# Five small reorderings in a fused neighbourhood-attention layer: square root's table, squares, held outputs, double loads, roots

## The chip, the cores and the metric

The kernel runs on one core of a Trainium2 chip. The metric is the device time of one execution in microseconds, the median over several runs. Engines are named as the profile names them: PE is TensorE (PEld its weight loads), DVE is VectorE, ACT is ScalarE, POOL is GpSimd, SP is the engine that issues most of the DMAs.

## The reference, cut to what matters

The reference has two kinds of layers, but with `DEPTH = 1` only the first one runs. All data is float32: `x` is 2048 tokens by 1024 features, there are 16 heads of 64, and the tokens form a grid of 32 rows by 64 columns.

```python
h = rmsnorm(x, norm_0)
q, k, v, gate = split(h @ w_in_0, 4)          # 1024 x 4096 weights
# each token attends to 8 rows x 16 columns around it, with a bias per head
s = q . k / sqrt(64) + rpb_0[head, row offset, column offset]
o = softmax(s) @ v
x = x + (o * silu(gate)) @ w_out_0            # 1024 x 1024 weights
out = rmsnorm(x, norm_f)
```

`rmsnorm(x, g)` is `x * rsqrt(mean(x*x) + 1e-6) * g`, so every token needs one inverse root at the beginning and one at the end.

## The kernel before, in words

Every float32 product is made of three products of a narrower float32 form: each operand is split into a high part (a copy on ACT) and a residual (a subtraction on DVE), and PE multiplies high by high, high by low and low by high. The large projections also use a scheme with seven instead of eight half-size products, so operands are first added and subtracted (`S1` to `S4` for weights, `T1` to `T4` for `x`) and results are combined again.

The instructions are issued in an order written out by hand; each engine works through its own list in that order, and an instruction waits until its operands and its buffer are ready. Buffers come from pools of fixed size: `ev` has 8, `mp` 10, `raw` 6. A buffer is handed out again when all that reads the old tile is done.

`stage_one` projects the tokens of column chunks 0 and 1 (512 tokens each). Its list is `seq`: product `i` is a pair (unit `n`, `P`), where a unit is 128 columns of keys, queries or gates, twice. `step(i)` issues the twelve matmuls of product `i` (L447), then `after` (L494), which reads the bank, and then what `on(i, ...)` has put down for this place. Products 0 to 11 are the `P` = 1 and 2 of six units. From product 12 on the other five products of each unit follow, with units taken in pairs:

- `add` (L457, its operation at L460) reads a bank to which a later product of the same unit adds: `P` = 7 adds to the bank of `P` = 6, and so has to wait until `add` has read it.
- `out_` (L462) makes a finished output `tmp` at L465 and multiplies it by `rb[c]` at L468, the inverse root of each token of chunk `c`, spread over the partitions. On DVE for units below 6, on POOL above. As long as `rb[1]` isn't there, outputs of chunk 1 are put on the list `held`; `scale_held` scales and stores them all. `give` (L363) stores an output through SP at L380 some matmuls later.
- `first_out(n)` (L743) makes the output of `P` = 2 of unit `n`, with an operation at L360.
- `forms(i)` makes the split of the weights for the products up to `i` (L429 on ACT, L430 on DVE); `seven.sum` makes `S1` to `S4` (L436). `sums4` (L741) and `split` (L543 and L544) make `T4`.

The inverse roots of a chunk come about like this. `load_rows` (L641) loads eight half rows of tokens on SP, `square_rows` squares them on ACT with a sum (L207), `stats` (L209) adds the sums on DVE (L212, L213), takes the square root on ACT (L149) and finishes it on DVE (L150 to L153). `diagonal` puts the four results of a partition on diagonals and splits them (with `late` on ACT at L225 and L229, the residual on DVE at L232), and `spread_rstd` multiplies a matrix of ones, `onesr`, with both parts on PE (L241, L242), which spreads them over all partitions, and copies the result to `rb[c]`.

ACT evaluates functions from a table that it has to load (ACT_TABLE_LOAD in the profile). Copies and squares run without a load of their own once a table is there.

Attention runs in 32 cycles, each with the transposes of one pair of heads and 512 tokens (`ph`, L1342), their copies `pta` (L1331 on DVE, L1333 on ACT), the scores of the next (`s`, L1287), and the products with the values (`o`, L1361). Between them `feed` issues matmuls of projections or, later, of the output projection (`po`, L1565 to L1569), so that PE has work. Within a cycle, once its attention weights are normalised (`normalise`, L1312 on DVE), some of these may be issued:

- `split_rows`, which splits one tile of 128 rows of attention outputs for the output projection (L1407 on ACT, L1408 on DVE, two each),
- `run_scales`, which multiplies finished rows with their inverse root (two operations at L1479 on DVE) and sends them to the output,
- `run_roots`, which makes the final inverse root of a finished tile by eight operations on one column (L1464 to L1471 on DVE). It isn't run where scaling was due in the same cycle (`behind`).

`add_rows` adds the residual to a finished output product (L1437 on DVE), with a square on ACT a few matmuls later (L1440). The last ten tiles of rows follow after attention in `rows_by_seven` (`py`, L1657).

Of the kernel before, what the change touches and what calls it, by code (L numbers as in the profile page):

```python
# [11 lines left out]
F32 = mybir.dt.float32  # L12
# [65 lines left out]
def build(ctx, tc, x, xr, xt, wg, bias, w_out, n0, nf, out):  # L78
# [59 lines left out]
    ones = one.tile([128, 128], F32, name="ones")  # L138
    nc.vector.memset(ones, 1.0)
    onesr = one.tile([128, 128], F32R, name="onesr")  # L140
    rt = one.tile([128, 16], F32, name="rt")
    rth = one.tile([128, 8], F32, name="rth")
    g0 = one.tile([128, NK], F32, name="g0")
# [270 lines left out]
    def seven_products(us, c0, X1, also):  # L414
        seq = [(n, P) for n in range(len(us)) for P in order7]
        last = len(us) - 1
        A, F, B, U = {}, {}, {}, {}
        made, held = [0], []

        def load_w(n, f, home=raw):  # L420
            A[n, f] = home([128, 512], F32, "raw")
            k, j = us[n]
            b = 512 * quarter[f]
            nc.sync.dma_start(A[n, f], wg[KINDS[k] + j, :, b:b + 512])

        def form(n, P):
            src = A[n, uses[P][0]]
            F[n, P] = t = wp([128, 2, 512], F32R, "f")
            nc.scalar.activation(t[:, 0], src, AF.Copy)  # L429
            nc.vector.tensor_tensor(t[:, 1], src, t[:, 0].bitcast(F32), OP.subtract)  # L430

        def sum_(n, f):
            a, b, o = {"S1": ("A21", "A22", OP.add), "S2": ("S1", "A11", OP.subtract),
                       "S3": ("A11", "A21", OP.subtract), "S4": ("A12", "S2", OP.subtract)}[f]
            A[n, f] = xp([128, 512], F32, "s") if f in ("S1", "S2") else A[n, {"S3": "A21", "S4": "A12"}[f]]
            nc.vector.tensor_tensor(A[n, f], A[n, a], A[n, b], o)  # L436

        def product(n, P):
            if P in (1, 6, 5):
                B[n, P] = bank(512, "pp")  # L440
                for Q in {1: (2,), 6: (7, 4), 5: (3,)}[P]:
                    B[n, Q] = B[n, P]
            x, t = X1[uses[P][1]], F.pop((n, P))
            for k in range(4):
                c = slice(k * 128, k * 128 + 128)
                for m in range(3):
                    nc.tensor.matmul(B[n, P], t[:, int(m == 2), c], x[k][int(m == 1)],  # L447
                                     start=P in (1, 6, 5) and k == 0 and m == 0, stop=k == 3 and m == 2,
                                     skip_group_check=True)
                    due(1)  # L450

        def keep(n, home=None):
            kind = us[n][0]
            U[n, 1] = home or ep([128, 512], F32, "p1")
            nc.scalar.activation(lay(kind, U[n, 1]), of(kind, B[n, 1]), AF.Copy)

        def add(n, i, P):  # L457
            kind = us[n][0]
            U[n, i] = xp([128, 512], F32, "u")
            nc.vector.tensor_tensor(lay(kind, U[n, i]), of(kind, B[n, P]), lay(kind, U[n, 1]), OP.add)  # L460

        def out_(n, a, c, P, u, then):  # L462
            kind, j = us[n]
            tmp = ev([128, 512], F32, "tmp")
            nc.vector.tensor_tensor(lay(kind, tmp), of(kind, B[n, P]), lay(kind, u), OP.add)  # L465
            def scale():
                if c0 == 0:
                    (nc.vector if n < 6 else nc.gpsimd).tensor_tensor(tmp, tmp, rb[c], OP.mult)  # L468

            if c0 == 0 and c not in rb:  # L470
                held.append(lambda: (scale(), give(kind, 2 * j + a, c, tmp)))
                return
            scale()
            then.append(lambda: give(kind, 2 * j + a, c, tmp))

        def scale_held():
            while held:
                held.pop(0)()

        def ahead(i, lead=6):  # L480
            n, j = divmod(i, 7)
            if j == 5 and n + 2 <= last:
                for f in ("A21", "A22", "A11"):
                    load_w(n + 2, f)
            if j == 0 and n + 1 <= last:
                load_w(n + 1, "A12")
            while made[0] < len(seq) and made[0] <= i + lead:
                form(*seq[made[0]])
                made[0] += 1
            f = {0: "S1", 1: "S2", 2: "S3", 4: "S4"}.get(j)  # L490
            if f and n + 1 <= last:
                sum_(n + 1, f)

        def after(n, P, then):  # L494
            kind, j = us[n]
            if P == 1:
                keep(n)
            elif P == 6:
                add(n, "2", 6)
            elif P == 2:  # L500
                if c0 == 0:
                    evac(kind, 2 * j, c0, B[n, 2], then)
                else:
                    then.append(lambda kind=kind, j=j, p=B[n, 2]: give(kind, 2 * j, c0, p, True))
            elif P == 7:
                add(n, "3", 7)
            elif P == 5:
                out_(n, 1, c0 + 1, 5, U[n, "3"], then)
            elif P == 4:
                out_(n, 1, c0, 4, U[n, 1], then)  # L510
            elif P == 3:
                out_(n, 0, c0 + 1, 3, U[n, "2"], then)

        def run():
            then = []
            for i, (n, P) in enumerate(seq):
                product(n, P)
                now, then = then, []
                after(n, P, then)
                for f in now:  # L520
                    f()
                ahead(i)
                also(n - last, i - 7 * n)
            for f in then:
                f()

        parts = SimpleNamespace(load=load_w, form=form, sum=sum_, product=product, keep=keep, after=after, scale_held=scale_held, B=B)
        return ahead, run, parts

# [86 lines left out]
    def stage_one():  # L616
# [24 lines left out]
        def load_rows(c, hs, p):  # L641
            for h in hs:
                t, j = 4 * c + h // 2, h % 2
                rows_in[t, j] = p([128, 512], F32, "row")
                nc.sync.dma_start(rows_in[t, j], xr[t * 128:t * 128 + 128, 512 * j:512 * j + 512])
# [55 lines left out]
        def on(i, f, *a):  # L701
            todo.setdefault(i, []).append((f, a))
# [44 lines left out]
        parts_ = slice(0, 256), slice(256, 512)  # L747
        load_v0(0, 0, 0, cols=parts_[0], by=nc.scalar)
        load_x(0, "x11", 0, land["x11"][0], parts_[0])
        nc.scalar.activation(onesr, ones, AF.Copy)  # L750
        load_v0(0, 1, 0, cols=parts_[0])
        load_x(0, "x11", 0, land["x11"][0], parts_[1])
        load_v0(0, 0, 0, cols=parts_[1])
# [54 lines left out]
        for n in (4, 5):  # L808
            seven.load(n, "A11")
        load_rows(1, range(4), ev)  # L810
        load_rows(1, range(4, 6), mp)
        for k in range(4, 8):
            first_values(k)
            split("B22", "x22", (k - 4,), "x22")
# [27 lines left out]
            for f in ("S1", "S2"):  # L842
                seven.sum(n, f)
        split("T2", "x11", (1, 2))
        square_rows(1, range(2))
        step(7)
        split("T2", "x11", (3,))
        square_rows(1, range(2, 4))
        load_rows(1, range(4, 8), ev)
        for n in range(2):  # L850
            seven.sum(n, "S3")
        step(8)
# [10 lines left out]
        step(11)  # L863
        sums4(0, 1)
        forms(15)
        for k in range(4):
            if k < 2:
                on(12 + k, sums4, k + 2)
            on(12 + k, split, "T4", "x21", (k,))
        on(12, square_rows, 1, range(4, 8))  # L870
        on(14, seven.sum, 0, "S4")
        on(14, first_out, 2)
        on(13, stats, 1)
        on(16, seven.sum, 1, "S4")
        on(16, first_out, 3)
        on(15, diagonal, 1, ev, True)
        on(17, spread_rstd, 1)
        on(18, seven.scale_held)

        def ask_pair(a):  # L880
            spot = mkp([128, 3, 512], F32, "raw")
# [908 lines left out]
    for m in range(cycles + 1):  # L1790
# [3 lines left out]
        if m:  # L1794
            due_here = []
            quiet[0] = True
            if a < 12 and m > 8 and m % 2:
                normalise(2 * m - 1, True, lambda: due_here.append(split_rows() or consume(1, turn=True)))
            else:
                normalise(2 * m - 1, True)  # L1800
            most, behind = 99 if a > 12 else 0 if rows_due() else 1, bool(rooted)
            run_scales()
            if not behind:
                run_roots(most)
            for k in range(3):
                if m == 1 and k == 2:
                    pass
                elif a > 12 or not any(due_here) and (k < 1 or k < 2 and m > 8 and m % 2 == 0):
                    got = split_rows()
                    due_here.append(got)  # L1810
                    if not got:
                        consume(1, turn=True)
                    elif a < 12 and m % 2 == 0 and len(items) - state["used"] == 8:
                        feed(a * 0.2)
                        consume(1, turn=True)
                feed(a * 0.2)
        else:
            feed(a * 0.6)
# [61 lines left out]
```

## Time and profile before

| | us |
|---|---|
| median of 3 runs | 1009.08 (1009.04 to 1009.55) |
| the profiled execution: time | 1008.7 |
| the profiled execution: span from the first to the last instruction | 1006.6 |
| PE busy in the span | 996.1 |
| DVE busy | 772.9 |
| ACT busy | 521.6 |
| POOL busy | 149.6 |

PE's granted clock is 0.998 of full speed. In the rows of the timeline the columns are the start in us from the beginning of the span, the length in us, the engine, the line, the operation, what it writes and reads, the shape and the count; in brackets stands how long the engine was idle before it, and what ended that. A group of rows that overlap, as they do on all engines, is shorter from start to start than its lengths add up to. In the rows of waits stand the engine that waited, its line, the engine and line that ended the wait, the total in us, how often, and the longest. In the rows of windows stand the stretch, its length, and the busy time of PE, PEld, DVE, ACT and POOL, then the clock, the DMA share and GB/s.

### The profile page before, as it was taken

To read this page: it belongs to the slowest core of one execution; us is meant where nothing else is said; L and a number is where in the kernel's file an instruction comes from. 1 tells how busy PE (TensorE), PEld (TensorE's weight loads), DVE (VectorE), ACT (ScalarE), POOL (GpSimd) and SP (SyncE) were. 2 spreads that over 40 slices of the span, in tenths; PEclk is the share of its full clock that TensorE was granted. 3 is DMA by queue.
4 is the path that set the end of the run, shared out by engine and by line. 5 is a ranking of instruction groups with operands and counts; after the bars stand their busy time and mean duration, and the time that the engine had idled before them with its cause. 6 is when DMAs were issued, how large, how long until landed. Compare 5 with 4: busy or idle time off the path is not lost.

```text
span 1006.6 us, 19545 instructions
## 1 busy us (share of the span) xinstructions
PE 996.1 (99%) x6904; PEld 796.8 (79%) x6904; DVE 772.9 (77%) x1703; ACT 521.6 (52%) x1272; POOL 149.6 (15%) x233
## 2 busy tenths in 40 slices
PE   9999999999999999999999999999999999999997
PEld 6887888888888888888888777777777777778886
DVE  5899888997666866676765676778788888887776
ACT  7872244455534423343433465677767657564443
POOL 0000001321100000000000133243333323222010
PEclk9999999999999999999999999999999999999999
DMA  8944447777957755655565797879888688799564
GB/s 282 357 116 164 136 139 251 245 244 256 366 146 226 250 149 176 209 189 178 209 199 199 213 276 228 266 236 291 276 254 266 192 252 275 231 354 361 121 176 115
DMA packets 150121, 228.18 MB, mean 227 GB/s; under 512 B 13640, under 2 KB 65096, under 8 KB 150024
## 3 DMA queue, kind: packets, MB, share of 16 engines
q1 hardware_dynamic: 147432, 222.61, 68.6%
q0 software_dynamic: 2160, 3.93, 2.3%
q8 instruction: 54, 0.88, 0.4%
q10 hardware_dynamic: 432, 0.40, 0.1%
q14 instruction: 43, 0.35, 0.1%
HBM read 160.83 MB, written 66.06 MB: 225 GB/s over the span
## 4 chain that ended last, share of the span: by engine, by line
PE 97%; ACT 1%; DVE 1%; DMA 1%; SPq 0%; issue 0%
PE pp L447 40%; PE pv L611 13%; PE py L1657 9%; PE o L1361 8%; PE s L1287 7%; PE ph L1342 4%; PE pp L393 2%; PE pv L726 2%; PE pp L395 2%; PE pp L391 2%; PE po L1565 2%; PE po L1567 2%; PE po L1569 2%; DMA em<-in_bias_dram 1%; ACT x L1302 0%; PE zp L135 0%
## 5 line engine op out<-in xcount | busy, mean ns | idle before, releaser
L447 PE MATMUL pp<-h,f 128*128 128x512 f32 x576 | 185.2, 389 | 0.0
L1314 POOL TENSOR_SCALAR x<-x,st 128x360 f32<-128x360 f32 (+5 forms) x192 | 106.4, 570 | 529.8 <-DVE st L1307 529.8
L447 PE MATMUL pp<-t,f 128*128 128x512 f32 x702 | 171.8, 389 | 1.3 <-ACT f L429 1.3
L447 PEld LDWEIGHTS pp<-t,f 128*128 128x128 f32 x702 | 131.7, 188 | 29.1 <-ACT f L429 1.6
L1302 ACT ACTIVATE x<-x,st 128x360 f32<-128x360 f32 (+5 forms) x256 | 134.2, 525 | 26.1 <-DVE st L1296 26.1
L447 PEld LDWEIGHTS pp<-h,f 128*128 128x128 f32 x576 | 108.1, 188 | 22.4
L447 PE MATMUL pp<-l,f 128*128 128x512 f32 x288 | 112.0, 389 | 0.0
L1296 DVE CUSTOM_DVE_ANT_0 x<-s,em 128x360 f32<-128x360 f32 (+5 forms) x256 | 102.6, 455 | 2.1 <-PE s L1287 1.3
L430 DVE TENSOR_TENSOR f<-raw,f 128x512 fp32r<-128x512 f32 x105 | 75.9, 727 | 19.9 <-ACT f L429 19.7
L1361 PEld LDWEIGHTS o<-pta,vt 120*64 120x64 f32 (+2 forms) x1024 | 68.7, 137 | 22.7 <-DVE st L1296 15.2
L1361 PE MATMUL o<-pta,vt 120*64 120x192 f32 (+5 forms) x1024 | 83.4, 316 | 0.3 <-issue 0.3
L429 ACT ACTIVATE f<-raw 128x512 fp32r<-128x512 f32 x105 | 63.3, 622 | 36.8 <-DVE raw L436 19.1
L1331 DVE COPY pta<-ph 120x512 f32<-120x512 f32 (+5 forms) x96 | 56.0, 638 | 32.1 <-PE ph L1342 31.9
L1287 PE MATMUL s<-kt,q 64*64 64x360 f32 (+5 forms) x1024 | 78.6, 420 | 1.2 <-ACT pta L1333 0.9
L1333 ACT ACTIVATE pta<-ph 120x512 f32<-120x512 f32 (+5 forms) x96 | 46.7, 557 | 62.7 <-PE ph L1342 62.6
L447 PEld LDWEIGHTS pp<-l,f 128*128 128x128 f32 x288 | 54.1, 188 | 11.3
L1287 PEld LDWEIGHTS s<-kt,q 64*64 64x64 f32 x1024 | 41.4, 131 | 23.1 <-ACT pta L1333 7.5
L611 PE MATMUL pv<-wh,t 128*128 128x512 f32 x176 | 56.2, 389 | 0.0
L447 PE MATMUL pp<-sixths,f 128*128 128x512 f32 x198 | 52.7, 389 | 0.0
L468 POOL TENSOR_TENSOR tmp<-tmp,rb 128x512 f32<-128x512 f32 x18 | 28.4, 1579 | 161.9 <-DVE tmp L465 131.0
L1342 PEld LDWEIGHTS ph<-ident,x 64*120 64x120 f32 (+2 forms) x1408 | 42.5, 128 | 11.3 <-issue 9.5
L1657 PE MATMUL py<-woh,f 128*128 128x512 f32 x160 | 50.6, 390 | 0.0
(225 smaller groups left out, 1873.5 us busy)
## 6 DMA issues: line engine op xcount, KB each, us to landing
raw<-in_wg_dram SPq DMA_DIRECT2D x124, 256.0 KB, 5.1
row<-in_xr_dram SPq DMA_DIRECT2D x34, 256.0 KB, 5.2
vd<-v SPq DMA_DIRECT2D x32, 256.0 KB, 3.3
sgd<-sg SPq DMA_DIRECT2D x32, 256.0 KB, 5.1
q<-qd SPq DMA_DIRECT2D x32, 256.0 KB, 5.8
sgt<-sgd SPq DMA_DIRECT2D x32, 256.0 KB, 6.6
ogd<-og SPq DMA_DIRECT2D x32, 256.0 KB, 3.9
kt<-kd SPq DMA_DIRECT2D x16, 480.0 KB, 6.3
```

The lines of the kernel that those rows point to most:

```text
L429: nc.scalar.activation(t[:, 0], src, AF.Copy)
L430: nc.vector.tensor_tensor(t[:, 1], src, t[:, 0].bitcast(F32), OP.subtract)
L447: nc.tensor.matmul(B[n, P], t[:, int(m == 2), c], x[k][int(m == 1)], start=P in (1, 6, 5) and k == 0 and m == 0, stop=k == 3 and m == 2, s ...
L611: nc.tensor.matmul(p, a[:, o], b, start=P in (1, 6, 5) and k == 0 and m == 0, stop=k == 3 and m == 2, skip_group_check=True)
L1287: nc.tensor.matmul(pst[s][h * 64:h * 64 + 64], qt[a, g * 64:g * 64 + 64], kt[a, :r1 - r0, c0:c0 + 8 * WIDE[C]].rearrange("p r (s c) -> p s ...
L1296: nc.vector.tensor_tensor_reduce(X[i, C][s], pst[s], EM[p, ROW_TYPE[T]][C > 0][s], -1.0, 1e38, OP.add, OP.min, st[:, o:o + 1])
L1302: nc.scalar.activation(X[i, C][s], X[i, C][s], AF.Exp, bias=st[:, o:o + 1], scale=-1.0, accum_out=st[:, 4 + o:5 + o])
L1314: nc.gpsimd.tensor_scalar(X[i, C][s], X[i, C][s], st[:, o:o + 1], 1.0, op0=OP.mult, op1=OP.mult)
L1331: nc.vector.tensor_copy(o, i_)
L1342: nc.tensor.transpose(ph[b, h][:k, o:o + 64], X[2 * m + late_, group[g]][s][q, at:at + k], ident[q, q])
L1361: nc.tensor.matmul(o[s * 64:s * 64 + 64, g0 * 64:g1 * 64], vt[:k, strip, s * 64:s * 64 + 64], t[:k, n * 64:(n + g1 - g0) * 64], start=stri ...
L1657: nc.tensor.matmul(B[m, P], t[:, a, c], b, start=P in (1, 6, 5) and k == 0 and i == 0, stop=k == 3 and i == 2, skip_group_check=True)
```

## The change

- The first activation of ACT is a square root of a single column of ones, in place of the copy that made `onesr`; that copy goes to DVE. So the table that is loaded first is the one of the square root.
- Two of the row loads of chunk 1 are dropped: the same half rows were loaded again later, and the first copies were never read.
- The squares of the first four half rows of chunk 1 move from behind products 6 and 7 to behind product 11, and the loads of the other four with them. The squares of these move from behind product 12 to 14, `stats` from 13 to 14, the diagonal from 15 to 16, the spreading from 17 to 18.
- All outputs of chunk 1 made before the list is emptied are held, whether `rb[1]` is there or not, and the list is emptied behind product 23 in place of 18.
- In attention no root is issued in a cycle in which rows were already split.

```diff
     onesr = one.tile([128, 128], F32R, name="onesr")
+    nc.vector.tensor_copy(onesr, ones)
...
-            if c0 == 0 and c not in rb:
+            if c0 == 0 and c == 1 and held is not None:
                 held.append(lambda: (scale(), give(kind, 2 * j + a, c, tmp)))
                 return
...
         def scale_held():
-            while held:
-                held.pop(0)()
+            nonlocal held
+            for f in held:
+                f()
+            held = None
...
-        nc.scalar.activation(onesr, ones, AF.Copy)
+        nc.scalar.activation(tiny.tile([128, 8], F32, name="t")[:, :1], ones[:, :1], AF.Sqrt)
...
         load_rows(1, range(4), ev)
-        load_rows(1, range(4, 6), mp)
...
         split("T2", "x11", (1, 2))
-        square_rows(1, range(2))
         step(7)
         split("T2", "x11", (3,))
-        square_rows(1, range(2, 4))
-        load_rows(1, range(4, 8), ev)
...
         forms(15)
+        square_rows(1, range(4))
+        load_rows(1, range(4, 8), ev)
...
-        on(12, square_rows, 1, range(4, 8))
+        on(14, square_rows, 1, range(4, 8))
         on(14, seven.sum, 0, "S4")
         on(14, first_out, 2)
-        on(13, stats, 1)
+        on(14, stats, 1)
         on(16, seven.sum, 1, "S4")
         on(16, first_out, 3)
-        on(15, diagonal, 1, ev, True)
-        on(17, spread_rstd, 1)
-        on(18, seven.scale_held)
+        on(16, diagonal, 1, ev, True)
+        on(18, spread_rstd, 1)
+        on(23, seven.scale_held)
...
             run_scales()
-            if not behind:
+            if not (behind or any(due_here)):
                 run_roots(most)
```

## The prediction

> **What bounds the kernel now.** I read the engine shares first, then the waits of TensorE, then the windows, and then the timelines of TensorE, VectorE and ScalarE around each wait.
>
> ```profile
> span 1006.6 us, 19545 instructions
> PE 996.1 (99%) x6904; PEld 796.8 (79%) x6904; DVE 772.9 (77%) x1703; ACT 521.6 (52%) x1272; POOL 149.6 (15%) x233
> PE pp L447 <- ACT f L429: 1.3, 1, 1.3
> PE zp L135 <- DVE z L132: 1.2, 1, 1.2
> PE s L1287 <- ACT pta L1333: 0.9, 2, 0.7
> PE s L1287 <- DVE y L1437: 0.2, 1, 0.2
> 77.00:98.00 21.00, 19.75 (x88) 15.98 (x87) 20.43 (x33) 7.00 (x12) 0.00 (x0) 1.00 0.40 142
> 1000.20:1006.60 6.40, 0.00 (x0) 0.00 (x0) 2.13 (x6) 2.09 (x7) 0.00 (x0) 0.73 0.43 164
> ```
>
> TensorE sets the time: it idles 1006.6 - 996.1 = 10.5 us. Of that 1.2 is the start and 6.4 the tail behind the last matmul, and the diff reaches neither. So about 2.9 us is all that any reordering can win, and a gain in VectorE or ScalarE counts only where it shortens one of two stalls. The kernel's 0.2%, about what a measurement can tell from no change, is 2.0 us.
>
> **The first stall**, in the first stage (TensorE rows, then VectorE, then ScalarE):
>
> ```profile
> 74.40 2.89 PE L447 MATMUL pp<-t,f 128*128 128x512 f32 x12
> 77.12 0.40 PE L241 MATMUL prb<-dgh,onesr 128*128 128x512 f32 x1
> 88.53 5.60 PE L447 MATMUL pp<-t,f 128*128 128x512 f32 x24
> 95.38 0.93 PE L447 MATMUL pp<-t,f 128*128 128x512 f32 x3 [1.25 <-ACT f L429]
> 85.14 1.29 DVE L468 TENSOR_TENSOR tmp<-tmp,rb 128x512 f32<-128x512 f32 x2
> 92.74 0.69 DVE L468 TENSOR_TENSOR tmp<-tmp,rb 128x512 f32<-128x512 f32 x1
> 94.55 0.69 DVE L460 TENSOR_TENSOR u<-pp,acc 128x512 f32<-128x512 f32 x1
> 87.07 0.63 ACT L429 ACTIVATE f<-raw 128x512 fp32r<-128x512 f32 x1 [4.51 <-DVE raw L436]
> ```
>
> One product is 12 matmuls and takes 77.12 - 74.40 = 2.72 us from start to start. Products 22 and 23 (counted in `seq`) start at 88.53, so 24 was due at 88.53 + 5.44 = 93.97 and came at 95.38: 1.41 us lost, of which the row shows 1.25, because the last matmuls' pipelined ends count as busy. The label names the split at L429, but counting the L429 rows in program order puts product 24's own split at 87.07, eight microseconds earlier. What did end just before 95.38 is L460, at 94.55 + 0.69 = 95.24: it reads the bank that product 22 filled and that product 24 adds to. It came late because VectorE was behind. So I take the stall as VectorE's queue, not as a missing operand.
>
> **The second stall**, in attention (VectorE, ScalarE, TensorE; then an earlier cycle with a late row sum but no root):
>
> ```profile
> 845.60 0.91 DVE L1408 TENSOR_TENSOR gl<-ograw,gh 128x512 fp32r<-128x512 f32 x1
> 846.42 0.20 DVE L1464 TENSOR_SCALAR st<-st 128x1 f32<-128x1 f32 x1
> 848.01 0.68 DVE L1437 TENSOR_TENSOR y<-po,xr 128x512 f32<-128x512 f32 x1
> 848.73 0.63 ACT L1440 ACTIVATE xr<-y 128x512 f32<-128x512 f32 x1 [3.77 <-DVE y L1437]
> 849.36 1.43 ACT L1333 ACTIVATE pta<-ph 96x512 f32<-96x512 f32 x3
> 846.78 0.39 PE L1569 MATMUL po<-wol,gh 128*128 128x512 f32 x1
> 848.75 0.54 PE L1287 MATMUL s<-kt,q 64*64 64x192 f32 x2 [0.22 <-DVE y L1437]
> 849.99 2.16 PE L1287 MATMUL s<-kt,q 64*64 64x192 f32 x30 [0.70 <-ACT pta L1333]
> 817.10 1.44 ACT L1333 ACTIVATE pta<-ph 120x512 f32<-120x512 f32 x3
> 817.73 2.17 PE L1287 MATMUL s<-kt,q 64*64 64x192 f32 x30 [0.19 <-ACT pta L1333]
> ```
>
> Here VectorE does a row split (L1408), then a root of eight tiny operations (L1464 to L1471, 846.42 to 848.01, 1.59 us), then the row sum L1437. The square L1440 waits for that sum, the copies L1333 are queued behind the square, and the scores wait for the copies.
>
> **The change, part by part.**
>
> *Held outputs scaled later.* Four outputs of column chunk 1 (products 15, 18, 19, 21) are multiplied by `rb[1]` at L468. Before, all four run ahead of the add at 94.55. Now they wait until the work after product 23, that is behind the adds of 22 and 23. Start to start such an operation takes 0.61 us (the pair at 85.14 takes 1.29 with its tail), so four are 2.4 us: the add runs at 94.55 - 2.4 = 92.1 and ends at 92.8, before product 24 is due at 93.97. The 1.41 us goes. What is late next: the four scalings then start at about 94.7 behind the add of product 23, which had to wait for its product anyway, and end at 97.1. The residual of product 28 and the add of product 24 follow by 99.0. That add is next needed by product 27, due at 93.97 + 3 × 2.72 = 102.1. The cover is 3 us, so I cost this at nothing. Four buffers of `ev`'s eight are held meanwhile. Counting allocations from product 14 on, the eighth is taken at product 21 and none is short.
>
> *Square root's table first.*
>
> ```profile
> 2.96 0.31 ACT L750 ACTIVATE onesr<-ones 128x128 fp32r<-128x128 f32 x1
> 3.75 0.29 DVE L567 CAST wh<-raw 128x256 fp32r<-128x256 f32 x1 [2.48 <-DMA raw<-in_wg_dram]
> 39.99 1.28 ACT L149 ACT_TABLE_LOAD   x1
> 40.89 0.17 DVE L213 TENSOR_SCALAR m<-m 128x4 f32<-128x4 f32 x1
> 41.28 0.20 ACT L149 ACTIVATE a<-m 128x4 f32<-128x4 f32 x1
> ```
>
> One load of 1.28 us leaves ScalarE at 39.99. But the root needs `m`, which VectorE finishes at 40.89 + 0.17 = 41.06; the table was ready at 41.27. So the chain gains 0.2 us, and ScalarE waits for most of the rest. At the start a copy of 0.31 us becomes a root of at most 0.20 us, and the copy goes to VectorE, which idles 2.48 us there: nothing either way. The Trainium skill (ScalarE: Activation LUTs, "What ACT_TABLE_LOAD costs") puts every switch of sets at about 1.28 us plus a drain of 1.38 us. The load itself agrees with 1.28, and the root starts directly behind it, so no drain shows; were all 2.66 us on TensorE's path, the sum below would be about 1003.8 instead of 1006.5, as an estimate from that page.
>
> *Second chunk's squares, and the double loads.*
>
> ```profile
> 63.40 0.63 ACT L543 ACTIVATE t<-spot 128x512 fp32r<-128x512 f32 x1 [3.81 <-DVE spot L741]
> 63.94 0.62 ACT L207 ACTIVATE row<-row 128x512 f32<-128x512 f32 x1
> 67.04 0.69 DVE L430 TENSOR_TENSOR f<-raw,f 128x512 fp32r<-128x512 f32 x1 [0.55 <-ACT f L429]
> 75.63 0.69 DVE L232 TENSOR_TENSOR dgl<-dg,dgh 128x512 fp32r<-128x512 f32 x1
> 79.96 0.68 DVE L436 TENSOR_TENSOR s<-raw 128x512 f32<-128x512 f32 x1
> DMA to landing us min/median/max: 3.9/5.2/7.1
> ```
>
> A square with its accumulator read is 0.61 us from start to start, four are 2.4. Four of them fall into ScalarE's 3.81 us idle stretch before 63.40; the other four move from product 12 to 14. VectorE's 0.55 us wait at 67.04, behind those squares, goes. With the 0.2 above VectorE is some 0.7 to 0.8 us earlier from there on. That helps no product by itself; it adds to the cover of the 92.1. Two loads that nothing reads leave SP's queue. The other four row loads move behind product 11, where SP has them wait until the squares free their buffers. The gap begins at 63.40 - 3.81 = 59.6, so the squares end by 62.0 and the loads are issued by about 62.5; at 3.9 to 7.1 us to landing they are there by 66.4 to 69.6. VectorE asks for their sums nine operations of 0.6 us after the one at 67.04, which is now at 66.3: at 71.7. So 1.5 us of cover stay behind the slowest landing and its square. Behind them on SP are two key stores, and loads that wait for VectorE's splits anyway: nothing.
>
> *Diagonal and broadcast one product later.* This is the new place where TensorE can wait directly: the broadcast needs `dgl`. The broadcast moves from 77.12 to 79.84, its second matmul to 80.1. `dgl` leaves 75.63 and goes behind the third `first_out`; what followed that one began at 79.96, so `dgl` starts at 79.96 - 0.60 (its old place, now free) - 0.8 = 78.6 and ends at 79.3. Cover 0.8 us, cost nothing.
>
> *No root beside a row split.* With the root gone from this cycle, the row sum waits for its last matmul, 846.78 + 0.39 = 847.17, ends at 847.9, the square ends at 848.55, and the copies start there instead of at 849.36. The scores follow the copies by 0.63 us (817.10 to 817.73, and 849.36 to 849.99), so they come at 849.18 instead of 849.99: 0.81 us won, and a short wait stays, as in the cycle at 817. From here roots and scalings alternate one cycle later:
>
> ```profile
> 856.37 1.65 DVE L1479 SCALAR_TENSOR_TENSOR y<-y,st,acc 128x512 f32<-128x512 f32 x2
> 909.68 1.41 DVE L1479 SCALAR_TENSOR_TENSOR y<-y,st,acc 128x512 f32<-128x512 f32 x2
> 924.11 0.69 DVE L1669 TENSOR_TENSOR u<-py,p 128x512 f32<-128x512 f32 x1 [1.50 <-PE py L1657]
> ```
>
> A root of 1.59 takes the place of a scaling of 1.65 and the other way round, so the following cycles keep their load. At the end one more row is scaled near 909.68, 1.4 us of VectorE, and its output stores go out later. VectorE idles 1.50 us before 924.11, and the stores are far from the tail: nothing.
>
> **Sum.** 1.41 + 0.81 = 2.22 us. Execution profiled: 1008.7 (span 1006.6 and 2.1 around it), so 1006.5. The median of the runs is 1009.08, 0.4 above that execution; I forecast 1009.08 - 2.2 = 1006.9. Buffers of `ev`, `mp` and `raw` are handed out in another order after this, which no row shows: I bound it by the largest late wait of TensorE, 0.7 us, either way, and take zero, as nearly all of the 6904 matmuls wait for nothing. The forecast's own range is 1006.2 to 1007.6.
>
> **The rivals.**
>
> *Only one stall goes.* If the label at 95.38 is right (the operand from L429), the first stays and only 0.81 is won: 1008.3. If the root's gap is filled by the next late thing, only 1.41: 1007.7. Against the first: the count of L429 rows and the 0.14 us between L460's end and the restart. Against the second: the same chain at 817 cost 0.19 without a root.
>
> *Nothing moves.* VectorE is busy for 20.43 of the 21 us from 77 to 98, so the stall could turn up at another bank a few products later: 1009.1. Against it: the 3 us of cover.
>
> *Slower: the broadcast waits for late row loads.* Last row's landing, square (0.7), mean (0.4), root and four small operations (1.1), diagonal (1.3), its copy (0.7), residual (0.7): 4.9 us to the broadcast's second matmul at 80.1. So TensorE waits one for one from a landing at 75.2. To end 2 us slower it must lose 4.2, a landing at 79.4: 1011.1. With the loads issued by 62.5 that is 17 us against 7.1 at most. It would need SP's queue to be held by a buffer that the new order frees late. The Trainium skill (DMA: Bandwidth & Descriptors, "Rules for kernel authors") advises to issue a transfer early and wait for it late, and moving these loads from 50 to 61 us goes against that. The landing row says the hidden time still suffices.
>
> *More goes*, the short waits left in attention too: 1006.0.
>
> **How the numbers follow.** Forecast 0.60; one stall 0.20; nothing 0.06; slower 0.11; more 0.03. The 0.2% line is at 1009.08 - 2.02 = 1007.06, just above my forecast. I give three quarters of the forecast's 0.60 to below it (0.45), plus 0.03: faster 0.48. The rest, 0.15 + 0.20 + 0.06, is within: 0.41. Slower 0.11. The range 1006.0 to 1008.8 holds the forecast, more, and one stall: 0.83.
>
> **What would show it.** The wait of `pp` at L447 is gone from TensorE's waits, with the add L460 of product 22 ended by 93, and four L468 rows in a run near 95. One ACT_TABLE_LOAD fewer at L149, and ScalarE waiting for `m` near 41. Squares in the former gap before 63. TensorE's wait at the scores near 848 down to 0.2 to 0.3. I am wrong if `prb` at L241 or L242 shows a wait, if the 1.3 us returns under another name before 110, or if VectorE waits for a store of `tmp`.

## The result, and the profile after

The kernel after takes 1005.92 us (median of 14 runs, 1005.01 to 1008.16), the kernel before beside it on the same chip 1008.73 us (14 runs, 1006.73 to 1011.12). The ratio is 0.9976, with a 95% interval of 0.9968 to 0.9983: about 2.4 us faster. The forecast was 1006.9 with a range of 1006.0 to 1008.8 and faster as the likeliest case. The median of 1005.92 itself lies 0.08 us under that range; but the kernel before also ran 0.35 us shorter beside it than the 1009.08 from which the forecast was counted. The difference, forecast as 2.2 us, came out as 2.4 by the ratio and 2.8 by the two medians. The profiled execution of after took 1005.34 us, that of before 1008.7, so between the two profiles there are 3.2 us of span to explain.

The page's first lines and TensorE's waits, after:

```profile
span 1003.4 us, 19549 instructions
PE 995.4 (99%) x6904; PEld 797.1 (79%) x6904; DVE 771.9 (77%) x1704; ACT 520.4 (52%) x1271; POOL 149.5 (15%) x233
```

```profile
PE zp L135 <- DVE z L132: 1.2, 1, 1.2
PE o L1362 <- issue: 0.3, 1, 0.3
PE s L1288 <- ACT pta L1334: 0.2, 1, 0.2
```

The busy times hardly changed. What went is waiting: the 1.3 us of `pp` and 0.9 of the 1.1 us of the scores. (Line numbers are one to three higher than before from L139 on, and differ by a few between the kernels below.)

**The first stall**, after (TensorE, then VectorE):

```profile
88.19 6.28 PE L448 MATMUL pp<-t,f 128*128 128x512 f32 x27
91.11 0.69 DVE L461 TENSOR_TENSOR u<-pp,acc 128x512 f32<-128x512 f32 x1 [0.56 <-PE pp L448]
93.83 0.69 DVE L461 TENSOR_TENSOR u<-pp,acc 128x512 f32<-128x512 f32 x1 [1.43 <-PE pp L448]
94.43 2.49 DVE L469 TENSOR_TENSOR tmp<-tmp,rb 128x512 f32<-128x512 f32 x4
98.04 0.68 DVE L461 TENSOR_TENSOR u<-pp,acc 128x512 f32<-128x512 f32 x1
```

Products 22, 23 and the start of 24 are now one row of 27 matmuls without a break. The add that product 24 needs starts at 91.11, right behind product 22, and it is now VectorE that waits 0.56 us for TensorE. The four scalings stand in one row behind the next add, as forecast for 94.7.

**The second stall**, after (TensorE, then VectorE, then ScalarE):

```profile
845.24 0.39 PE L1570 MATMUL po<-wol,gh 128*128 128x512 f32 x1
845.56 1.43 PE L1343 MATMUL ph<-ident,x 64*96 64x64 f32 x44
846.92 2.37 PE L1288 MATMUL s<-kt,q 64*64 64x192 f32 x32
843.41 1.50 DVE L1409 TENSOR_TENSOR gl<-ograw,gh 128x512 fp32r<-128x512 f32 x2
844.84 0.68 DVE L1438 TENSOR_TENSOR y<-po,xr 128x512 f32<-128x512 f32 x1
845.54 0.64 ACT L1441 ACTIVATE xr<-y 128x512 f32<-128x512 f32 x1 [2.16 <-DVE y L1438]
846.30 1.46 ACT L1334 ACTIVATE pta<-ph 96x512 f32<-96x512 f32 x3
```

All 32 scores follow the transposes in one row. The row sum (L1438) runs right behind the row split, 0.4 us before the last output matmul at 845.24 even begins.

**Where the 3.2 us went**, by how much earlier each place starts in the profile after: first product of the first stage 0.35 (it starts at 16.40 and at 15.98 in the two profiles of after, so a difference of this size is not put down to the change); product 24 another 1.40; up to the first attention cycle another 0.11; a cycle near 690 gives 0.3 back; the cycle near 846 another 1.33; the tail 0.3 shorter.

### The profile page after: what moved, and what is told of

It is laid out like the page before. It is cut to its first block, busy times and chain, and to the rows that moved or that the text cites. A ratio compares the mean times of both kernels' runs of the same rounds, so it can differ in the third digit from the quotient of the medians.

```text
span 1003.4 us, 19549 instructions
## 1 busy us (share of the span) xinstructions
PE 995.4 (99%) x6904; PEld 797.1 (79%) x6904; DVE 771.9 (77%) x1704; ACT 520.4 (52%) x1271; POOL 149.5 (15%) x233
## 4 chain that ended last, share of the span: by engine, by line
PE 99%; ACT 1%; DVE 0%; issue 0%
PE pp L448 40%; PE pv L614 13%; PE py L1658 10%; PE o L1362 8%; PE s L1288 7%; PE ph L1343 4%; PE pp L394 2%; PE po L1566 2%; PE pv L729 2%; PE po L1568 2%; PE pp L396 2%; PE pp L392 2%; PE po L1570 2%; ACT x L1303 0%; PE zp L135 0%; PE prb L242 0%
```

## The experiments

Twelve runs. "Before" is the median of the kernel before on the same chip; the waits are TensorE's in the profiled execution.

| kernel | median (runs' extremes) | before | ratio, 95% interval | `pp` waits | scores wait |
|---|---|---|---|---|---|
| held_only | 1006.99 (1006.42–1007.61) | 1008.45 | 0.9981, 0.9972–0.9991 | none | 1.1 |
| root_only | 1007.42 (1005.55–1009.09) | 1008.45 | 0.9986, 0.9975–0.9997 | 1.1 | 0.2 |
| order_only | 1007.07 (1006.69–1009.27) | 1008.45 | 0.9988, 0.9977–0.9999 | 0.2 | 0.9 |
| table_only | 1007.82 (1007.12–1009.0) | 1008.45 | 0.9992, 0.9983–1.0002 | 1.7 | 1.1 |
| all_but_held | 1008.1 (1005.28–1011.28) | 1008.27 | 0.9999, 0.9986–1.0013 | 0.2 | 0.2 |
| all_but_root | 1007.14 (1006.37–1008.87) | 1008.27 | 0.9993, 0.9984–1.0001 | none | 1.1 |
| forms_earlier | 1008.86 (1008.17–1010.93) | 1008.27 | 1.0009, 1.0001–1.0018 | 1.7 | 1.1 |
| loads_first | 1005.65 (1005.2–1011.63) | 1008.27 | 0.9985, 0.9972–0.9998 | none | 0.2 |
| after_again | 1005.07 (1004.89–1010.35) | 1008.58 | 0.9979, 0.9963–0.9994 | none | 0.2 |
| late_sends | 1005.16 (1004.89–1005.49) | 1008.58 | 0.9967, 0.9955–0.9980 | none | 0.2 |
| og_first | 1005.82 (1005.08–1009.87) | 1008.58 | 0.9974, 0.9961–0.9988 | none | 0.2 |
| all_but_table | 1005.56 (1004.74–1011.69) | 1008.58 | 0.9977, 0.9963–0.9992 | none | none |

### One part alone

`held_only`: the kernel before with the held outputs' part.

```diff
-            if c0 == 0 and c not in rb:
+            if c0 == 0 and c == 1 and held is not None:
...
-        on(18, seven.scale_held)
+        on(23, seven.scale_held)
```

> The kernel before with one part of the change: outputs of chunk 1 held until product 23. Theory (VectorE's queue in front of the add L460 of product 22 is the first stall): 2.4 us of scalings go from ahead of that add, product 24 starts when it is due, the stall of 1.41 us is gone, the one in attention stays; 1.4 us faster. Rival (product 24 waits for its split operand L429, as the label says): the split isn't touched, the wait of 1.25 us stays; 0 us.

`root_only`: the kernel before with the guard on the root.

```diff
-            if not behind:
+            if not (behind or any(due_here)):
```

> The kernel before with one part of the change: no root beside a row split. By the prediction 0.8 us faster, with a short wait left at the scores. By what the two traces show (the row sum's product had ended before the last matmuls ahead of the transposes, so square and copies aren't late at all) 1.3 to 1.4 us faster, no wait left at the scores of that cycle, and the wait of 1.25 us in the first stage unchanged.

`order_only`: the kernel before with the moved squares, row loads, `stats`, diagonal and broadcast, and without the double loads.

```diff
-        load_rows(1, range(4, 6), mp)
...
+        square_rows(1, range(4))
+        load_rows(1, range(4, 8), ev)
...
-        on(15, diagonal, 1, ev, True)
-        on(17, spread_rstd, 1)
+        on(16, diagonal, 1, ev, True)
+        on(18, spread_rstd, 1)
```

> The kernel before with squares, row loads, sums, diagonal and broadcast moved and the double loads dropped, but the table as before, outputs of chunk 1 held only until rb[1] is there, and roots as before. Theory: by the trace after, VectorE comes to the add of product 22 some 1.2 us earlier by these moves alone, and the scalings are still ahead of it: of the 1.41 us of the first stall 0.1 to 0.4 are left, 1.0 to 1.3 us faster. Rival (the parts add up, and only the held outputs matter): stall unchanged, 0 us.

`table_only`: the kernel before with the first activation a square root.

```diff
+    nc.vector.tensor_copy(onesr, ones)
...
-        nc.scalar.activation(onesr, ones, AF.Copy)
+        nc.scalar.activation(tiny.tile([128, 8], F32, name="t")[:, :1], ones[:, :1], AF.Sqrt)
```

> The kernel before with one part of the change: square root's table first, onesr made on VectorE. Theory: ScalarE waits for the mean instead of for the table, VectorE gains 0.2 us near 41, which shortens the first stall by at most 0.2 us; time within 0.2 us. Rival (a load of 1.28 us less on a busy ScalarE shifts all that follows): VectorE 1.3 us earlier, the first stall down to 0.1 us, 1.3 us faster.

TensorE's waits, of `held_only` (two rows) and `root_only` (two rows), then the row of `order_only`'s timeline in which product 24 starts:

```profile
PE s L1289 <- ACT pta L1335: 0.9, 2, 0.7
PE s L1289 <- DVE y L1439: 0.2, 1, 0.2
```

```profile
PE pp L447 <- ACT f L429: 1.1, 1, 1.1
PE s L1287 <- ACT pta L1333: 0.2, 1, 0.2
```

```profile
94.00 0.93 PE L447 MATMUL pp<-t,f 128*128 128x512 f32 x3 [0.17 <-ACT f L429]
```

The two stalls are separate: the held part takes all of the first and none of the second, the guard the other way round. But two parts work on the first one. The moves alone, with the scalings still ahead of the add, leave a wait of 0.17 us: product 24 starts 0.33 us late instead of 1.41, because the add of product 22 runs at 93.17 instead of 94.55. The moves bring VectorE to the add earlier, the held part takes the scalings out of its way; the held part suffices alone, the moves almost. In medians the four parts alone won 1.5, 1.0, 1.4 and 0.6 us, 4.5 together, and the whole change 2.4 by the ratio and 2.8 by the medians. The first stall's 1.4, which two parts each take, and the table's 0.6, whose interval reaches past no change, make up the difference. The table alone removes no wait. Its 1.7 beside 1.3 before is no loss: the first stage started 0.7 us earlier in that profile, while product 24 started within 0.2 us of where it did.

### One part left out

`all_but_held`, `all_but_root` and later `all_but_table` are the kernel after with one of these diffs undone.

> The changed kernel without the held outputs (scaled at once when rb[1] is there, the list emptied behind product 18). Theory: the moves of squares and sums alone bring VectorE to the add of product 22 early enough to leave only 0.1 to 0.4 us of the first stall; 2.4 to 2.7 us faster than before. Rival (parts add up): the stall of 1.41 us is back in full; 1.3 us faster.

> The changed kernel without the guard on roots. Theory: the first stall is gone, the cycle near 846 has its waits of 0.2 and 0.7 us back; 1.4 us faster than before, 1.3 to 1.4 slower than with the guard. Rival (the guard only delays the same work): as fast as the changed kernel.

The waits are as the single parts had them: without the guard the scores wait 1.1 us again, without the held part product 24 waits 0.2. But the medians don't fit them. `all_but_root` won 0.7 us by the ratio, with an interval that reaches no change, where 1.4 was expected. `all_but_held` should have lost some 0.2 us against after and lost about 2: its runs lie in two groups, 1005.3 to 1007.0 and 1009.2 to 1011.3. So something else lengthens some executions, and both profiles name a new wait, of `py`, 0.2 and 0.6 us, at a place that neither edit touches. That is followed below.

### Which label is right

`forms_earlier`: the kernel before, with the weight splits behind products 19 to 23 issued one product earlier. The edit moves the splits of products 25 to 29; that of product 24 is behind product 19 in both kernels. So the operand that the label names is made as early as before, while one more split of VectorE stands ahead of the add. If product 24 waits for its operand, nothing changes; if it waits for VectorE's queue, it comes later.

```diff
-            forms(i + (4 if i < 17 else 5 if i < 33 else 6))
+            forms(i + (4 if i < 17 else 6 if 19 <= i < 24 else 5 if i < 33 else 6))
```

> The kernel before, with the splits of the weights (L429, L430) put one product earlier in the order behind products 19 to 23. Theory: product 24's split was done long ago; one more split of 0.6 us is now ahead of the add of product 22 on VectorE, the stall grows from 1.4 to about 2.0 us; 0.6 us slower. Rival (product 24 waits for L429): its operand is there earlier, the stall shrinks or goes; up to 1.4 us faster.

```profile
86.64 0.63 ACT L429 ACTIVATE f<-raw 128x512 fp32r<-128x512 f32 x1 [4.51 <-DVE raw L436]
94.72 0.68 DVE L460 TENSOR_TENSOR u<-pp,acc 128x512 f32<-128x512 f32 x1
95.55 0.94 PE L447 MATMUL pp<-t,f 128*128 128x512 f32 x3 [1.71 <-ACT f L429]
```

Product 24 came at 95.55 where 93.68 was due, 1.87 us late instead of 1.41. Its own split (the first row) was done 8 us before, as in the kernel before, and the restart again follows the end of the add (95.40) by 0.15 us. The expectation's rival, that the operand would be there earlier, was not tested by this edit, since that operand did not move; but `held_only` removed the whole wait without touching any split. So the label "ACT f L429" did not name what was missing. It was VectorE's add.

### A new wait of VectorE near 103

After, VectorE waits twice in the first stage for weight loads, which I had not foreseen (VectorE, then SP):

```profile
102.94 0.69 DVE L437 TENSOR_TENSOR s<-raw 128x512 f32<-128x512 f32 x1 [2.26 <-DMA raw<-in_wg_dram]
106.17 0.69 DVE L437 TENSOR_TENSOR s<-raw 128x512 f32<-128x512 f32 x1 [0.61 <-DMA raw<-in_wg_dram]
95.14 0.92 SPq L381 DMA_DIRECT2D kd<-tmp  x2
96.16 1.38 SPq L425 DMA_DIRECT2D raw<-in_wg_dram  x3
```

SP issues the next three weight loads behind two stores of outputs that were held, and four more behind the other two stores. In `all_but_held`, which lacks the held part, these loads start at 94.20 instead of 96.16 and VectorE's sum at 100.81 waits for nothing. `loads_first` registers the emptying of the list behind these loads.

```diff
-        on(23, seven.scale_held)
...
+        on(23, seven.scale_held)
         for n in range(E, len(us)):
```

> The changed kernel, with the loads of unit 4's weights behind product 23 ahead of the stores of the held outputs on SP's queue, not behind them. Theory: in the trace after, VectorE waits 2.26 us at 103 for these loads, which SP issues behind stores of scaled outputs; with the loads ahead that wait goes or falls under 0.5 us, and the time stays (within 0.2 us), as TensorE has cover there. Rival (that wait eats VectorE's cover and is felt later): 0.3 us or more faster than the changed kernel.

```profile
100.32 0.68 DVE L437 TENSOR_TENSOR s<-raw 128x512 f32<-128x512 f32 x1
104.40 0.69 DVE L437 TENSOR_TENSOR s<-raw 128x512 f32<-128x512 f32 x1 [1.46 <-DMA raw<-in_wg_dram]
```

```profile
PE py L1658 <- DVE y L1438: 2.2, 2, 1.6
PE py L1658 <- ACT f L1624: 1.0, 1, 1.0
```

The first sum now waits for nothing (100.32), as expected; the wait of the second one grew from 0.61 to 1.46 us, while VectorE asks 2.6 us earlier (102.94 instead of 105.56). TensorE feels these waits in neither kernel, so nothing was won there: the shorter half of the executions of `loads_first` (1005.2 to 1005.7) is like that of after. The profiled execution, though, was one of the long ones, 1009.25 us, and shows where time is lost in it: 3.2 us at `py`, after attention (the last two rows).

### The late wait after attention

In that execution and in after, VectorE's first sum of the third pair of rows waits for its loads (`loads_first`, then after, with SP's stores and loads ahead of it; then SP in before):

```profile
936.92 0.69 DVE L1631 TENSOR_TENSOR s<-raw 128x512 f32<-128x512 f32 x1 [9.71 <-DMA raw<-ogd]
```

```profile
930.96 0.69 DVE L1631 TENSOR_TENSOR s<-raw 128x512 f32<-128x512 f32 x1 [3.68 <-DMA raw<-ogd]
916.25 2.80 SPq L1484 DMA_DIRECT2D out_dram<-y  x4
919.50 19.65 SPq L1619 DMA_DIRECT2D raw<-ogd  x6
```

```profile
918.89 1.05 SPq L1483 DMA_DIRECT2D out_dram<-y  x2
920.22 21.82 SPq L1618 DMA_DIRECT2D raw<-ogd  x6
```

The guard moves the scaling of one row to the end of attention, and with it two more output stores of 256 KB to SP's queue just ahead of these loads. Relative to the first `py` product the loads start 17.7 us after it instead of 15.6. Two kernels test it, with the kernel after once more as the yardstick on the same chip.

> The kernel after once more, unchanged, as the yardstick of the other three on the same chip. Theory: its executions spread upwards because VectorE's first sum of the third row pair (s<-raw, L1631, near 927) waits for loads that SP issues behind four stores of outputs; the wait was 3.7 us in the profile of 1005.34 us and up to 9.7 us in a kernel whose profiled execution took 1009.25 us. Expected: a median of 1005.3 to 1006.5, lowest near 1005.0, single executions up to 1008; the wait at L1631 is there, 2 to 8 us. Rival (the spread comes from somewhere else): L1631 waits no longer in a slow execution than in a fast one.

`late_sends`: the kernel after, with these stores planned later, behind the third pair's two loads.

```diff
-            store(("y", n), 18, send)
+            store(("y", n), 100 if ended[0] else 18, send)
```

> The kernel after, with the four output stores of rows 4 and 5 planned 100 instead of 18 products behind their scaling: SP then issues the two loads of the third row pair's sum ahead of them. Theory: these loads start at about 916.3 instead of 919.5, with four stores fewer ahead of them, and land by about 925; VectorE asks at 927.3, so its wait at L1631 falls from 3.7 us to under 1 us, TensorE's waits for py go where there are any, and the executions draw together: median 1005.0 to 1005.5, highest under 1007. Rival one (the landing of the held output's store, ogd<-og, holds SP, as the chain of the slow execution has it): L1631 waits within 1 us as in the kernel after. Rival two (the stores pushed back now stand ahead of the next four loads): the wait moves to the fourth pair's sums near 945 and the median stays or rises by up to 1 us.

`og_first`: the last store of attention's outputs ahead of seven weight loads instead of behind them; the four output stores stay where they are.

```diff
+        while any(e[1][0] == "og" for e in later):
+            later.pop(0)[2]()
         land_T4()
```

> The kernel after, with the last store of gated values (ogd<-og) issued ahead of the seven loads of out-projection weights (sixths, t) instead of behind them; the four output stores stay ahead of the loads. It tells what holds the third pair's loads. Theory (SP's queue order and the stores' traffic): that store starts 4.5 to 5 us earlier, near 911, but the loads raw<-ogd still start at 919 to 920 and L1631 still waits 2 to 8 us; median within 0.5 us of the kernel after's. Rival (SP stands until ogd<-og has landed, as the chain of the slow execution has it): the loads start and land earlier, L1631 waits under 1 us and the median is as with the stores put back, 1005.0 to 1005.5.

`after_again` (an execution of 1004.89 us), `late_sends` and `og_first`:

```profile
918.25 20.43 SPq L1619 DMA_DIRECT2D raw<-ogd  x6
927.74 0.69 DVE L1631 TENSOR_TENSOR s<-raw 128x512 f32<-128x512 f32 x1 [0.92 <-DMA raw<-ogd]
```

```profile
917.22 1.02 SPq L1619 DMA_DIRECT2D raw<-ogd  x2
918.48 3.00 SPq L1484 DMA_DIRECT2D out_dram<-y  x4
927.57 0.68 DVE L1631 TENSOR_TENSOR s<-raw 128x512 f32<-128x512 f32 x1
```

```profile
911.13 0.52 SPq L1369 DMA_DIRECT2D ogd<-og  x1
917.85 2.85 SPq L1484 DMA_DIRECT2D out_dram<-y  x4
920.80 19.93 SPq L1619 DMA_DIRECT2D raw<-ogd  x6
933.05 0.69 DVE L1631 TENSOR_TENSOR s<-raw 128x512 f32<-128x512 f32 x1 [5.56 <-DMA raw<-ogd]
```

In `late_sends` the two loads start 15.1 us after the first `py` product, land 6.0 us after their issue, and VectorE waits neither here nor at the sums of the fourth pair, so the second rival of `late_sends` falls. In the other kernels with the guard, the moves and the held outputs the four stores are ahead of these loads, and the median landing of the six was 7.4 us (`after_again`), 9.4 (after), 10.1 (`all_but_table`, without the table's part), 10.2 (`og_first`) and 12.3 (`loads_first`). In `og_first` the other store starts 4.5 us earlier and the wait is there all the same, 5.56 us, so the landing of that store is not what holds the loads: the first rival falls by this run.

But the two additional stores are not shown to be what opens the wait. `root_only` has all four ahead of the loads and no wait; `all_but_root` has two, as before, and waits 6.87 us:

```profile
917.33 2.63 SPq L1483 DMA_DIRECT2D out_dram<-y  x4
928.54 0.68 DVE L1630 TENSOR_TENSOR s<-raw 128x512 f32<-128x512 f32 x1
```

```profile
919.98 1.89 SPq L1484 DMA_DIRECT2D out_dram<-y  x2
935.47 0.69 DVE L1631 TENSOR_TENSOR s<-raw 128x512 f32<-128x512 f32 x1 [6.87 <-DMA raw<-ogd]
```

What goes with the long waits, over all fourteen profiles, is how late SP is before it comes to the output stores. The last weight load ahead of them (`t<-wodT`) starts 15.1 to 16.0 us after the first `py` product in the five profiles that wait 5.56 us or more, and 13.0 to 14.4 us after it in the nine that wait 3.68 us or less. No run here shows what makes SP late there.

TensorE feels the wait only beyond some 6 us. VectorE's wait for these loads and TensorE's wait at `py` were: up to 5.56 and none (ten profiles), 6.21 and 0.2 (`all_but_held`), 6.87 and 0.6 (`all_but_root`), 6.98 and 0.6 (`all_but_table`), 9.71 and 3.2 (`loads_first`). In these four, all of the wait but 6.0 to 6.5 us is passed on. This is read off different kernels; no run varies the wait alone. It would explain why after loses some of its 2.4 us again in some executions, but none of its longer ones was profiled.

The lists of runs leave another cause open. Among the twelve kernels of the table, twelve executions took more than 1009.8 us. Eight of these list a granted clock of 0.996 or 0.997, and all other executions 0.998 to 1.000. By an estimate from these numbers, a clock lower by 0.002 makes TensorE's 995 us 2 us longer. Whether the lower clock lengthens these executions or comes from their waits is not shown; the profiled one of `loads_first` lost its 3.2 us at 0.999.

`late_sends` has no such wait in its profile and is no slower than after: 0.9967 [0.9955, 0.9980] beside 0.9979 [0.9963, 0.9994] for `after_again`. Its median is that of `after_again` (1005.16 and 1005.07), but its five runs lie within 0.6 us, where two of seven of `after_again` were at 1007.95 and 1010.35. That no long execution is left is not shown by five runs, and one profile without the wait is little, as `root_only` has one too. The kernel before spreads as well, 1006.78 to 1012.61 beside these runs, without this wait in its profile and at clocks of 0.998 and 0.999. The cause of that stays open. So does what makes the landings differ between executions of one program.

### The table left out

> The kernel after without its first part: the square root's table is loaded where the first square root stands, and onesr is copied by ScalarE again. Theory: the table alone was worth 0.9992 of the time [0.9983, 1.0002], no product waits for it, so the median is within 0.4 us of the kernel after's; the first root runs near 40 behind its load and still waits for the maximum, and product 24 does not wait (no more than 0.2 us). Rival one (the table is part of the cover): product 24 waits 0.2 to 0.6 us and the median is that much later. Beside it: in the attention cycle near 690 the scores' 32 products took 2.79 us and ScalarE's copies began 0.27 us later in every kernel that has both the table and the moves, 2.52 us in those with one of them; without the table 2.52 us is expected if the two together make it, 2.79 us if the moves alone do.

Its profile (ScalarE near 40 and near 690), then the same two places after:

```profile
39.36 1.28 ACT L149 ACT_TABLE_LOAD   x1
40.65 0.20 ACT L149 ACTIVATE a<-m 128x4 f32<-128x4 f32 x1
689.18 1.47 ACT L1333 ACTIVATE pta<-ph 120x512 f32<-120x512 f32 x3 [0.98 <-PE ph L1342]
689.85 2.51 PE L1287 MATMUL s<-kt,q 64*64 64x240 f32 x32
```

```profile
40.11 0.20 ACT L150 ACTIVATE a<-m 128x4 f32<-128x4 f32 x1 [1.12 <-DVE m L214]
689.88 1.47 ACT L1334 ACTIVATE pta<-ph 120x512 f32<-120x512 f32 x3 [1.25 <-PE ph L1343]
690.27 2.79 PE L1288 MATMUL s<-kt,q 64*64 64x240 f32 x32
```

The median of 1005.56 is within 0.5 of `after_again`'s, the intervals of the ratios cover each other, and product 24 does not wait. So the table's part wins nothing that can be measured, alone or with the rest. Against the expectation the root waited here for its load, which ended at 40.64, and not for `m`, which was finished at 40.42. The 0.3 us that the cycle near 690 gives back is there in every kernel with both the table's part and the moves, and in none with one of them; what in them delays three copies some 600 us later stays open.

## Why the prediction was right, point by point

- **The number.** It fits better than its working: the two stalls gave 2.73 us where 2.22 was forecast, and places that the forecast did not have gave 0.3 back (near 690) or added 0.3 (the tail).
- **The bound.** Right: TensorE's busy time moved by 0.7 us, and what was won is two stalls.
- **First stall.** Right in size and cause: 1.41 us forecast, 1.40 measured. The working gave the held part all of the credit, with the add at 92.1. It came at 91.11, of which the earlier start explains 0.35: VectorE had caught up entirely and waited 0.56 us for the product. I had put the moves down as cover alone; `order_only` shows that they take 1.08 of the 1.41 us by themselves.
- **Second stall: mis-sized**, 0.81 forecast, 1.33 measured. The step that failed is "the row sum waits for its last matmul, 846.78 + 0.39". Its product had ended earlier: the sum ran at 844.84, before that last matmul began. So nothing was left of the chain square, copies, scores, and the short wait that I kept, as at 817, went too. The rows of before could not show it, since the root's eight operations stood between the split and the sum; I took the nearest matmul for its producer without counting which bank the sum reads.
- **Table.** Right: costed at 0.2 us off the path. After, the root waits 1.12 us for `m`, so most of the load's 1.28 us only became idle time. In `all_but_table` the load is in place, and the root starts 0.01 us behind its end. The Trainium skill (ScalarE: Activation LUTs, "What ACT_TABLE_LOAD costs") adds a drain of 1.38 us to each switch of sets; by that rule the part would be worth 2.66 us of ScalarE, and no run shows more than the load.
- **Squares and row loads.** Right that they don't show: the first four squares run from 58.31, the second four without waiting for a load, and VectorE's sums of chunk 1 run at 71.22 where 71.7 was forecast. VectorE gained some 1.0 to 1.2 us rather than 0.7 to 0.8: in `order_only` the split that stood at 81.29 runs at 80.04, and its first product started 0.3 us earlier.
- **Diagonal and broadcast.** Right: `dgl` ended at 78.75 (79.3 forecast), and neither broadcast matmul waited.
- **SP's queue: missed.** "I cost this at nothing" held for TensorE in the first stage, but stores of held outputs now stand ahead of weight loads, and VectorE waits 2.26 and 0.61 us. For the end, "its output stores go out later … nothing" asked whether the stores come near the tail and not which loads stand behind them on SP. Waits of up to 9.71 us turned up there, of which TensorE got at most 3.2. They come with the guard and without it, so how much of them is due to the later stores stays open.
- **The slower rival** named a late row load in the first stage. The mechanism, loads held behind something else on SP, did turn up, in another place. The Trainium skill (DMA: Bandwidth & Descriptors, "Rules for kernel authors") says to issue early and wait late; the moved row loads that it speaks against were harmless here, and `late_sends`, which moves two loads ahead by 2.3 us, is where the rule agrees with a profile: VectorE's wait for them, 3.68 us in after, is none.

## What to carry to other kernels

When a stall is a queue, find which operation ended just before the restart, whatever the label says, and expect several edits that empty that queue to share one gain instead of adding. When a step is moved, ask for each of its stores which loads stand behind it on the issuing queue, and how much wait the engine that needs them can take before TensorE feels it. A spread of runs that grows after a change is worth a profile of a long execution: it showed a wait that the median hid. Before a part of the change is blamed for such a wait, look for it in the profiles of the kernels that have only this part, and of those that have all but it.

## What the runs showed of the hardware

Loads of 256 KB from SP's queue at the same place took a median of 6.0 us to land when issued ahead of the four output stores (`late_sends`), 6.9 to 11.4 behind two stores (six kernels), and 6.4 to 12.3 behind four (seven kernels); the number of stores does not put them in order. The table loads took 1.28 us each, and where the function's operand was there, it started 0.01 to 0.02 us behind the load's end (39.99 before; 198.81 and 253.34 after).
